# A gated recurrence's units: outputs formed beside the next unit, transposed two units later, preparation in place

## The chip, the cores and the metric

The kernel runs on one core of a Trainium2 chip. The metric is the device time of one execution in microseconds (us); the time before is the median of three runs. One further execution was profiled, and all rows of the profile come from that one.

## What is computed

One layer of a hybrid diffusion backbone over 1024 latent and 256 context tokens: a modulated norm, one input projection, two token mixers beside each other (a bidirectional gated linear recurrence and attention), gates, an output projection, and a feed-forward block. The change touches the recurrence (four heads of 128 keys by 128 values, chunks of 32 tokens, forward and backward):

```python
def hgrn_scan(q, k, v, log_f, s0):               # k = 1 - f, f = exp(log_f)
    a = jnp.cumsum(log_f, axis=3)                # within a chunk of 32 tokens
    a_last = a[:, :, :, -1]
    q_dec = q * jnp.exp(a)
    k_dec = k * jnp.exp(-a)
    scores = jnp.where(mask, jnp.einsum('bhnik,bhnjk->bhnij', q_dec, k_dec), 0.0)
    o_intra = jnp.einsum('bhnij,bhnjv->bhniv', scores, v)
    k_end = k * jnp.exp(a_last[:, :, :, None, :] - a)
    kv = jnp.einsum('bhnck,bhncv->bhnkv', k_end, v)
    decay = jnp.exp(a_last)
    ...                                          # scan over chunks: s = decay * s + kv
    o_inter = jnp.einsum('bhnck,bhnkv->bhncv', q_dec, s_starts)
    o = (o_intra + o_inter)...
    return o, s_final
...
    o = o_f + flip(o_b)                          # both directions
    o = rms_norm(o, norm_w) * jax.nn.silu(heads(hg))
```

The context's scan starts from a zero state, the latents' scans from a given one.

## The kernel before

The stages follow each other: front (norm, q/k/v), attention with a part of the input projection as filler, the recurrence stage with the gate projection as filler (735 to 1077 us in the profile), the merge, the output projection, and the feed-forward block. The order of TensorE's (PE's) instructions is the order in which the code is written; the order on the other engines, and which free buffer a tile gets, is set by a scheduler. An engine carries out its own instructions in order, so one that waits holds all behind it. SyncE (SP) issues nearly all DMAs, also in order.

The recurrence stage is a loop over 24 units (`HUnit`): for each head six pairs of a direction d and a token tile t: (0,0), (0,1), (1,1), (1,0), (0,2), (1,2). Tiles 0 and 1 have 512 tokens (four blocks of 128), tile 2, the context, has 256. Units are counted here from 0, so 6, 12 and 18 begin a head, and the two before each of these are short. A turn of the loop handles unit u:

- `prep` of unit u+1, a turn ahead: loads (`uf` the gate f, `uq`, `uv`, and `ug` for d = 1), k = 1 - f on GpSimd (POOL, L837), two scans on VectorE (DVE, L841 to L846), a dozen tiny products for the chunk factors `um` (L856 to L865), then k times the second scan (POOL, `usf`, L875), the keys `uke` for the state (DVE, L871), the keys for the scores (POOL), and the four scaled queries `uw` (two on DVE, two on POOL).
- `keys_t` (L890): PE transposes `uke`, ScalarE (ACT) copies it to `ukt`. `scores` (L900): 16 or 32 small products, then the mask on DVE (`usm`, L903) and for d = 1 an addition on POOL. `states_` (L911): PE forms kv, DVE chains the states `ust` (L917), four steps for a long unit.
- `out` (L927, L929): PE multiplies the queries `uw` with the states `ust`, and for d = 1 the scores with v. For d = 1, DVE adds the forward part (`uo`, L939), ACT squares, POOL forms the power, and DVE scales (L946). `out_t` (L952): the transpose of `uo`, one unit later in the code.
- Between these stand slices of the filler (`part(x)`): steps of the gate projection (L299 to L301, three products of 512 columns each) and of the modulation (`ada_cols`), whose result DVE adds into `modc` (L190). A unit's slice of the filler is in proportion to its tokens.

Unit u's `ust`, and so its `out`, come in the same turn in which DVE prepares unit u+1. The preparation's tiles lie in ring "X", 20 buffers of 2 KB per partition, 11 or 12 for a unit.

Of the kernel before, what the change touches and what calls it, by code (L numbers as in the profile page):

```python
# [44 lines left out]
def build(ctx, tc, I, O, C):  # L45
# [128 lines left out]
    def ada_cols(pa, ws, cis, ring=None):  # L174
# [8 lines left out]
        s_.activation(ev, pa[:, 0:256], AF.Copy)  # L183

        def late():
            pm = pa[:, 256:260]
            for half, ci in enumerate(cis):
                pe.matmul(pm[:, 2 * half:2 * half + 2], ev[:, half * P:(half + 1) * P], sel, start=True, stop=True)
            for half, ci in enumerate(cis):
                v.tensor_tensor(modc[:, :, ci], pm[:, 2 * half:2 * half + 2],  # L190
                                cols[:, B_ADA + ci:B_ADA + ci + 1].broadcast_to([P, 2]), op=ALU.add)
        return late


# [622 lines left out]
    class HUnit:  # L817
# [6 lines left out]
            self.zero = None if t < 2 else 0 if d == 0 else self.nb - 1  # L824

        def prep(self):
            h, d, t, n, nb = self.h, self.d, self.t, self.n, self.nb
            f, q, vv = S(name="uf"), S(name="uq"), S((P, 4, P), name="uv")
            self.vv = vv
            dma(f[:, 0:n], FD[d][h][t])  # L830
            dma(q[:, 0:n], QD[h][t])
            dma(vv[:, 0:nb, :], VD[h // 2][t][:, :, (h % 2) * P:(h % 2 + 1) * P])
            if d == 1:
                self.gt = S((P, 4, P), name="ug")
                dma(self.gt[:, 0:nb, :], GD[h // 2][t][:, :, (h % 2) * P:(h % 2 + 1) * P])
            k = S(name="uk")
            g_.tensor_scalar(k[:, 0:n], f[:, 0:n], -1.0, 1.0, op0=ALU.mult, op1=ALU.add)  # L837

            c, e = S(name="ucp"), S(name="usf")
            if d == 0:  # L840
                v.tensor_tensor_scan(c[:, 0:n], R[:, 0:n], f[:, 0:n], 1.0, op0=ALU.max, op1=ALU.mult)  # L841
                v.tensor_tensor_scan(e[:, 0:n - 1][:, ::-1], f[:, 1:n][:, ::-1], R[:, 1:n], 1.0, op0=ALU.mult, op1=ALU.max)
                v.memset(e[:, n - 1:n], 1.0)
            else:
                v.tensor_tensor_scan(c[:, 0:n][:, ::-1], R[:, 0:n], f[:, 0:n][:, ::-1], 1.0, op0=ALU.max, op1=ALU.mult)
# [10 lines left out]
            v.tensor_copy(out=Mf[:, 0:nb, 1:12:5], in_=Dv[:, :, 0:3])  # L856
            v.tensor_tensor(Mf[:, 0:nb, 2:8:5], Dv[:, :, 0:2], Dv[:, :, 1:3], op=ALU.mult)
            v.tensor_tensor(M[:, 0:nb, 0, 3], M[:, 0:nb, 0, 2], Dv[:, :, 2], op=ALU.mult)

            v.tensor_copy(out=M[:, 0:nb, 3, 2], in_=Dv[:, :, 3])  # L860
            for cc in (1, 0):
                v.tensor_tensor(M[:, 0:nb, 3, cc], M[:, 0:nb, 3, cc + 1], Dv[:, :, cc + 1], op=ALU.mult)
            v.reciprocal(M[:, 0:nb, 4, :], Dv)
            self.dec = T(4, "udec")
            v.tensor_tensor(self.dec[:, 0:nb], M[:, 0:nb, 3, 0], Dv[:, :, 0], op=ALU.mult)  # L865

            def mul4(out, in0, w, eng):
# [3 lines left out]
                eng.tensor_tensor(out[:, 0:n].rearrange("p (b c i) -> p b c i", c=4, i=32),  # L871
                                  in0[:, 0:n].rearrange("p (b c i) -> p b c i", c=4, i=32),
                                  mm.unsqueeze(3).broadcast_to([P, nb, 4, 32]), op=ALU.mult)
# [33 lines left out]
        def states_(self, st):  # L907
            nb = self.nb
            kv = PS("s", (P, 4, P))
            for b in range(nb):  # L910
                pe.matmul(kv[:, b, :], self.kts[:, b, :], self.vv[:, b, :], start=True, stop=True)  # L911
            self.states = {}
            nxt = S((P, 4, P), name="ust")
            for i, b in enumerate(list(range(nb)) if self.d == 0 else list(range(nb))[::-1]):
                self.states[b] = st
# [1 line left out]
                v.scalar_tensor_tensor(dst, st, self.dec[:, b:b + 1], kv[:, b, :], op0=ALU.mult, op1=ALU.add)  # L917
# [37 lines left out]
            dma(OH[self.h][self.t], e[:, 0:nb].rearrange("p b d -> p (b d)"))  # L955

    def hgrn(fill):
        zs = cp.tile([P, P], F32, name="zs")
        g_.memset(zs, 0.0)
        units = [HUnit(h, d, t) for h in range(4) for d, t in ((0, 0), (0, 1), (1, 1), (1, 0), (0, 2), (1, 2))]  # L960
        st, fwd, late = None, {}, None
        tot = float(sum(u.n for u in units))
        done = 0.0
        units[0].prep()
        for i, u in enumerate(units):
            if i + 1 < len(units):
# [1 line left out]
            if u.t == 2:
                st = zs
            elif u.t == u.d:  # L970
                st = cp.tile([P, P], F32, tag="s0", name="s0", bufs=1)
                dma(st, I["state_hgrn"][u.d, u.h])
            if u.d == 0:
                fwd[u.t] = u
# [15 lines left out]
            if u.t == 2:  # L990
                dma(O["new_state_hgrn"][u.d, u.h], st)
            if u.d == 1:
                late = u
        late.out_t()
# [19 lines left out]
    def with_ada(gens, b0):  # L1014

        for i, gen in enumerate(gens):
            for j, x in enumerate(gen):
                if j == 6 and todo:
                    todo.pop()()
                yield x  # L1020
            if b0 + i < 16:
                raw = wraw(I["w_ada"], KC, 2 * D + (b0 + i) * 256)
                ci = 16 + 2 * (b0 + i)
                todo.append(ada_cols(PS("g"), [lambda k, h=h: raw[:, k, h * P:(h + 1) * P] for h in range(2)], (ci, ci + 1)))
                yield 1.8
# [633 lines left out]
```

## Time and profile before

| | |
|---|---|
| median of three runs | 2169.72 us (2169.2 to 2173.08) |
| profiled execution, its own time | 2168.73 us |
| its span, first to last instruction | 2167.0 us |
| recurrence stage | 735 to 1077 us of the span |
| mean granted TensorE clock | 0.987 |

In rows of the profile, "busy" is the time in which an engine executed, "idle before" the gap ahead of an instruction with what ended it, xN a number of instructions, and L927 a line of the kernel. PEld is PE's weight load, which runs beside its products; PEclk is the share of the full TensorE clock that was granted. Waits are put down to what came last by the semaphore events.

### The profile page before, as it was taken

How to read it: one execution, taken by the hardware profiler on the slowest of the kernel's cores; microseconds unless marked ns; L12 is line 12 of the kernel's file. 1: busy time of each engine (PE TensorE's matmuls, PEld its weight loads, DVE VectorE, ACT ScalarE, POOL GpSimd, SP SyncE). 2: the span in 40 equal slices, each digit the busy share in tenths (PEclk: the TensorE clock that was granted, in tenths of full speed). 3: DMA queues.
4: the chain of work that ended last, by engine and by line, in shares of the span. 5: the costliest groups of instructions: out<-in, count | busy, mean ns of one | idle time of the engine just before them, and what ended most of it. 6: DMA issues, size and time to landing. Idle time of an engine off the chain costs nothing.

```text
span 2167.0 us, 34635 instructions
## 1 busy us (share of the span) xinstructions
PE 2080.5 (96%) x12859; PEld 1789.1 (83%) x12859; DVE 1399.6 (65%) x2668; ACT 954.8 (44%) x1947; POOL 527.6 (24%) x554
## 2 busy tenths in 40 slices
PE   6899999999999999899999999899999999999998
PEld 4788889988899877787888888888888878888876
DVE  3784776677776877678443535966666665666675
ACT  4754555555555522222230425755454444333352
POOL 1472323333333454446212100112111110000010
PEclk9999999999999999999999999999999999999999
DMA  9365121242122344445544333674444478555773
GB/s 283 103 193 158 65 74 39 73 133 69 51 76 69 114 147 148 128 143 164 194 134 136 114 107 116 207 226 141 156 146 151 136 283 269 178 185 172 229 229 104
DMA packets 251065, 316.38 MB, mean 146 GB/s; under 512 B 18168, under 2 KB 171328, under 8 KB 250896
## 3 DMA queue, kind: packets, MB, share of 16 engines
q1 hardware_dynamic: 238768, 274.53, 40.3%
q0 software_dynamic: 12128, 39.64, 5.1%
q8 instruction: 101, 1.65, 0.3%
q14 instruction: 68, 0.56, 0.1%
HBM read 226.55 MB, written 87.56 MB: 145 GB/s over the span
## 4 chain that ended last, share of the span: by engine, by line
PE 75%; DVE 11%; DMA 6%; ACT 3%; issue 3%; SPq 1%; POOL 1%; DVEq 0%; POOLq 0%; ACTq 0%
PE ps_g L299 7%; PE ps_g L300 7%; PE ps_g L301 7%; PE ps_s L658 4%; PE ps_t L699 3%; DMA wraw<-in_w_in 3%; PE ps_s L1479 2%; PE ps_s L1480 2%; PE ps_g L1480 2%; PE ps_s L1481 2%; PE ps_g L1481 2%; PE ps_g L1479 2%; PE ps_s L1317 2%; PE ps_s L1319 2%; PE ps_s L1318 2%
## 5 line engine op out<-in xcount | busy, mean ns | idle before, releaser
L299 PE MATMUL ps_g<-hs,wsp 128*128 128x512 f32 (+1 forms) x960 | 361.0, 376 | 2.5 <-DVE modc L190 2.5
L301 PE MATMUL ps_g<-hs,wsp 128*128 128x512 f32 (+1 forms) x960 | 344.5, 359 | 0.0
L300 PE MATMUL ps_g<-hs,wsp 128*128 128x512 f32 (+1 forms) x960 | 344.3, 359 | 0.0
L677 POOL TENSOR_SCALAR pexp<-pexp,rs 128x512 f32<-128x512 f32 (+1 forms) x104 | 170.1, 1641 | 368.9 <-ACT pTh L702 179.1
L270 ACT ACTIVATE wsp<-wraw 128x1024 fp32r<-128x1024 f32 x118 | 118.2, 1001 | 270.7 <-PE ps_g L300 114.0
L271 DVE TENSOR_TENSOR wsp<-wraw,wsp 128x1024 fp32r<-128x1024 f32 x118 | 140.9, 1194 | 123.5 <-ACT wsp L270 123.1
L299 PEld LDWEIGHTS ps_g<-hs,wsp 128*128 128x128 f32 x960 | 184.0, 192 | 27.6 <-issue 4.8
L301 PEld LDWEIGHTS ps_g<-hs,wsp 128*128 128x128 f32 x960 | 183.5, 191 | 27.8
L300 PEld LDWEIGHTS ps_g<-hs,wsp 128*128 128x128 f32 x960 | 184.4, 192 | 19.9
L702 ACT ACTIVATE pTh<-ps_t 128x512 fp32r<-128x512 f32 x200 | 118.9, 601 | 132.4 <-PE ps_t L699 129.4
L659 DVE TENSOR_REDUCE mx<-ps_s 128x1 f32<-128x512 f32 (+1 forms) x208 | 136.7, 662 | 52.1 <-PE ps_s L658 51.5
L270 ACT ACTIVATE ah<-ar 128x640 fp32r<-128x640 f32 (+1 forms) x112 | 81.0, 723 | 197.6 <-PE ps_g L1451 192.5
L669 ACT ACTIVATE pexp<-ps_s,ngm 128x512 f32<-128x512 f32 (+1 forms) x208 | 137.3, 669 | 45.2 <-DVE ngm L663 43.7
L703 DVE TENSOR_TENSOR pTl<-ps_t,pTh 128x512 fp32r<-128x512 f32 x200 | 135.8, 679 | 13.1 <-ACT pTh L702 12.7
L271 DVE TENSOR_TENSOR ah<-ar,ah 128x640 fp32r<-128x640 f32 (+1 forms) x112 | 89.8, 802 | 74.1 <-ACT ah L270 72.7
L658 PE MATMUL ps_s<-Kl,Ql 128*128 128x512 f32 (+1 forms) x416 | 129.1, 415 | 2.3 <-ACT pexp L669 2.3
L699 PE MATMUL ps_t<-ident,pexp 128*128 128x128 f32 x800 | 120.6, 272 | 3.0 <-DVE pTl L703 1.7
L315 PE MATMUL ps_g<-wsp,hs 128*128 128x256 f32 x400 | 117.1, 293 | 0.0
L316 PE MATMUL ps_g<-wsp,hs 128*128 128x256 f32 x400 | 113.6, 284 | 2.8 <-DVE wsp L271 2.8
L317 PE MATMUL ps_g<-wsp,hs 128*128 128x256 f32 x400 | 113.7, 284 | 0.0
L715 PE MATMUL ps_g<-pTl,Vl 128*128 128x256 f32 x400 | 105.6, 286 | 4.5 <-DVE pTl L703 4.5
L714 PE MATMUL ps_g<-pTh,Vl 128*128 128x256 f32 x400 | 105.5, 284 | 0.2 <-DVE ze L810 0.2
(385 smaller groups left out, 5350.9 us busy)
## 6 DMA issues: line engine op xcount, KB each, us to landing
ar<-AF SPq DMA_DIRECT2D x112, 320.0 KB, 3.3
wraw<-in_w_ff SPq DMA_DIRECT2D x32, 1024.0 KB, 6.0
wr<-in_w_ff SPq DMA_DIRECT2D x128, 256.0 KB, 3.7
wraw<-in_w_in SPq DMA_DIRECT2D x19, 1024.0 KB, 6.5
wraw<-in_w_ada SPq DMA_DIRECT2D x16, 1024.0 KB, 5.4
AF<-a POOLq DMA_DIRECT2D x48, 256.0 KB, 2.7
AF<-t POOLq DMA_DIRECT2D x48, 256.0 KB, 2.3
wa<-in_w_ada SPq DMA_DIRECT2D x32, 256.0 KB, 5.8
```

Of the source, the lines that this page charges most:

```text
L270: s_.activation(hi, raw, AF.Copy)
L271: v.tensor_tensor(lo, raw, f32(hi), op=ALU.subtract)
L299: pe.matmul(out, hi[:, k, :], mh, start=(first and k == 0), stop=False)
L300: pe.matmul(out, hi[:, k, :], ml, start=False, stop=False)
L301: pe.matmul(out, lo[:, k, :], mh, start=False, stop=(last and k == kcs - 1))
L658: pe.matmul(pq[:, 0:n], self.qh[:, q0:q0 + P], K[self.g][var][self.kts[i]], start=(var == 0), stop=(var == 1))
L659: v.tensor_reduce(self.mx[j][:, i:i + 1], pq[:, 0:n], axis=AX.X, op=ALU.max)
L669: s_.activation(e[:, 0:n], self.ps.pop((j, i))[:, 0:n], AF.Exp, bias=self.mx[j], accum_out=self.sm[j][:, i:i + 1])
L677: NORM[(i + j) % len(NORM)].tensor_scalar(x, x, self.rs[j], None, op0=ALU.mult)
L699: pe.transpose(pt[:, a, j * P:(j + 1) * P], self.Ps[j][i][:, b * P:(b + 1) * P], ident)
L702: s_.activation(hi, pt, AF.Copy)
L703: v.tensor_tensor(lo, pt, f32(hi), op=ALU.subtract)
```

## The change

1. `out` of unit u-1 stands behind `states_` of unit u, and `out_t` of unit u-3 just ahead of it; the loop runs three turns longer.
2. `prep` is in place: k overwrites `uf` and is formed on ACT behind both scans; `uke` overwrites `usf`, and so waits for POOL's product that reads it; the fourth query overwrites `uq`. A unit has 8 or 9 tiles in ring "X"; `uv` and `ug` are loaded later in the preparation.
3. The filler is shared by tokens plus 128, and the three extra turns get 300 each, so that less stands between a unit's steps and some stands in the extra turns. The four places of a turn get a quarter each.
4. For the zero state, DVE copies kv in place of a product with a zero tile. The given states have two buffers, `oT` moves to ring "I", and within the two fillers `modc` is added by ACT.

```diff
@@ ada_cols (late) @@
-                v.tensor_tensor(modc[:, :, ci], pm[:, 2 * half:2 * half + 2],
-                                cols[:, B_ADA + ci:B_ADA + ci + 1].broadcast_to([P, 2]), op=ALU.add)
+                if on_act:
+                    s_.activation(modc[:, :, ci], pm[:, 2 * half:2 * half + 2], AF.Identity, bias=cols[:, B_ADA + ci:B_ADA + ci + 1])
+                else:
...
@@ HUnit.prep @@
-            f, q, vv = S(name="uf"), S(name="uq"), S((P, 4, P), name="uv")
+            f, q = S(name="uf"), S(name="uq")
...
-            k = S(name="uk")
-            g_.tensor_scalar(k[:, 0:n], f[:, 0:n], -1.0, 1.0, op0=ALU.mult, op1=ALU.add)
...
+            k = self.k = f
+            s_.activation(k[:, 0:n], f[:, 0:n], AF.Identity, scale=-1.0, bias=1.0)
...
             g_.tensor_tensor(e[:, 0:n], k[:, 0:n], e[:, 0:n], op=ALU.mult)
-            self.ke = S(name="uke")
-            mul4(self.ke, e, 3, v)
             mul4(k, e, 4, g_)
-            self.k = k
+            mul4(e, e, 3, v)
+            self.ke = e
...
-            W[3] = S(name="uw")
-            v.tensor_tensor(W[3][:, 0:n], q[:, 0:n], c[:, 0:n], op=ALU.mult)
+            W[3] = q
+            v.tensor_tensor(q[:, 0:n], q[:, 0:n], c[:, 0:n], op=ALU.mult)
             for w, eng in ((2, g_), (1, g_), (0, v)):
+                if w == 0:
+                    self.vv = S((P, 4, P), name="uv")
+                    dma(self.vv[:, 0:nb, :], VD[h // 2][t][:, :, (h % 2) * P:(h % 2 + 1) * P])
...
@@ HUnit.states_ @@
-                v.scalar_tensor_tensor(dst, st, self.dec[:, b:b + 1], kv[:, b, :], op0=ALU.mult, op1=ALU.add)
+                if b == self.zero:
+                    v.tensor_copy(out=dst, in_=kv[:, b, :])
+                else:
+                    v.scalar_tensor_tensor(dst, st, self.dec[:, b:b + 1], kv[:, b, :], op0=ALU.mult, op1=ALU.add)
@@ hgrn @@
+        N, LATE = len(units), 3
+        share = [u.n + 128.0 for u in units] + [300.0] * LATE
+        tot, done, st = sum(share), 0.0, None
         units[0].prep()
-        for i, u in enumerate(units):
-            if i + 1 < len(units):
+        for i in range(N + LATE):
+            part = lambda x: fill.to((done + x * share[i]) / tot)
+            if i + 1 < N:
                 units[i + 1].prep()
...
-            part = lambda x: fill.to((done + x * u.n) / tot)
-            u.keys_t()
-            part(0.2)
-            u.scores(fwd[u.t])
-            part(0.4)
-            u.states_(st)
-            st = u.last
-            part(0.7)
-            if late is not None:
-                late.out_t()
-                late = None
-            part(0.8)
-            u.out(fwd[u.t])
-            done += u.n
-            fill.to(done / tot)
+            if i < N:
+                u = units[i]
+                u.keys_t()
+                part(0.25)
+                u.scores(u.fwd)
+                part(0.5)
+                u.states_(u.st or st)
+                st = u.last
+                if u.t == 2:
+                    dma(O["new_state_hgrn"][u.d, u.h], st)
+                part(0.75)
+            if i >= LATE and units[i - LATE].d == 1:
+                units[i - LATE].out_t()
+            if 1 <= i <= N:
+                units[i - 1].out(units[i - 1].fwd)
+            part(1.0)
+            done += share[i]
```

PE, unit 10 (the forward context unit of the second head), before: from its kv product (its states go to `ust_11125`) to its own output product in the same turn.

```order
L911 MATMUL ps_s_11122<-uv_10865,ukt_11093 128x128 x2
L299 MATMUL ps_g_11128<-hs_736,wsp_10999 128x512
L300 MATMUL ps_g_11128<-hs_737,wsp_10999 128x512
L301 MATMUL ps_g_11128<-hs_736,wsp_11000 128x512
L299 MATMUL ps_g_11128<-hs_746,wsp_10999 128x512
L300 MATMUL ps_g_11128<-hs_747,wsp_10999 128x512
L301 MATMUL ps_g_11128<-hs_746,wsp_11000 128x512
L299 MATMUL ps_g_11128<-hs_756,wsp_10999 128x512
L300 MATMUL ps_g_11128<-hs_757,wsp_10999 128x512
L301 MATMUL ps_g_11128<-hs_756,wsp_11000 128x512
L952 MATMUL ps_t_11138<-ident_85,uo_11030 128x128 x4
L927 MATMUL ps_g_11146<-ust_11125,uw_10897 128x128
```

PE, the same product now (unit 10's states are `ust_11016` there, L921 is `states_`, L965 `out_t`, L940 `out`, and L302 to L304 are the filler):

```order
L921 MATMUL ps_s_11129<-uv_10952,ukt_11099 128x128 x2
L302 MATMUL ps_g_11026<-hs_714,wsp_11022 128x512
L303 MATMUL ps_g_11026<-hs_715,wsp_11022 128x512
L304 MATMUL ps_g_11026<-hs_714,wsp_11023 128x512
L302 MATMUL ps_g_11142<-hs_736,wsp_11022 128x512
L303 MATMUL ps_g_11142<-hs_737,wsp_11022 128x512
L304 MATMUL ps_g_11142<-hs_736,wsp_11023 128x512
L965 MATMUL ps_t_11146<-ident_85,uo_10888 128x128 x4
L940 MATMUL ps_g_11154<-ust_11016,uw_10806 128x128
```

The kv product ahead of it (`ps_s_11129`) is unit 11's: unit 10's output has moved a whole turn behind its own states.

DVE, the first unit's keys at the start of the stage, before (L703 and L724 belong to the end of attention, L271 to the filler's weights; the row of `uke_9518` is unit 0's keys, `ucp_9537` the first scan of unit 1):

```order
L871 TENSOR_TENSOR uke_9518<-usf_9502,um_9506 128x512
L882 TENSOR_TENSOR uw_9521<-uq_9494,ucp_9501 128x512
L703 TENSOR_TENSOR pTl_9413<-ps_t_9407,pTh_9412 128x512
L724 TENSOR_TENSOR oa_9424<-ps_g_9419,pvt_9425 64x256
L871 TENSOR_TENSOR uw_9527<-uw_9521,um_9506 128x512
L271 TENSOR_TENSOR wsp_9765<-wraw_9574,wsp_9764 128x1024
L724 TENSOR_TENSOR oa_9424<-ps_g_9440,pvt_9445 64x256
L841 SCALAR_TENSOR_TENSOR ucp_9537<-R_9488,uf_9529 128x512
```

DVE now (unit 0's keys are the row that writes `usf_9496`):

```order
L706 TENSOR_TENSOR pTl_9413<-ps_t_9407,pTh_9412 128x512
L865 TENSOR_TENSOR udec_9510<-um_9501,ucp_9495 128x4
L727 TENSOR_TENSOR oa_9424<-ps_g_9419,pvt_9425 64x256
L838 SCALAR_TENSOR_TENSOR ucp_9530<-R_9488,uf_9526 128x512
L839 SCALAR_TENSOR_TENSOR usf_9531<-uf_9526,R_9488 128x511
L840 MEMSET usf_9531 128x1
L274 TENSOR_TENSOR wsp_9759<-wraw_9566,wsp_9758 128x1024
L856 COPY um_9536<-ucp_9530 128x4x3
L857 TENSOR_TENSOR um_9536<-ucp_9530 128x4x2
L727 TENSOR_TENSOR oa_9424<-ps_g_9440,pvt_9445 64x256
L871 TENSOR_TENSOR usf_9496<-usf_9496,um_9501 128x512
```

The keys of unit 0 have moved behind both scans of unit 1 and a weight split.

DVE, the change of head, where unit 6's keys (`usf_10221`) stand now: behind the first scan of unit 7 (`ucp_10327`), which waits for that unit's gate to arrive. Before, each unit's keys stood ahead of the next unit's scan.

```order
L871 TENSOR_TENSOR uw_10247<-uq_10217,um_10226 128x512
L862 TENSOR_TENSOR um_10226<-um_10226,ucp_10220 128x4
L952 TENSOR_TENSOR uo_10188<-ps_g_10179,uo1_9780 128x512
L838 SCALAR_TENSOR_TENSOR ucp_10327<-R_9488,uf_10323 128x512
L163 TENSOR_SCALAR ms_10197<-oss_10190 128x4
L871 TENSOR_TENSOR usf_10221<-usf_10221,um_10226 128x512
```

The keys have moved behind one scan here, at the heads of units 6 and 18; at unit 12 they still stand ahead of the next scan.

More of the change, by code (lines that the diff above doesn't have):

```diff
@@ L172, in build, with ada_cols @@
     v.tensor_reduce(sel, ident.rearrange("p (j r) -> p r j", r=32)[:, 0:2, :], axis=AX.X, op=ALU.add)
-    def ada_cols(pa, ws, cis, ring=None):
+    def ada_cols(pa, ws, cis, ring=None, on_act=False):
         for half in range(2):
@@ L189, in late @@
             for half, ci in enumerate(cis):
-                v.tensor_tensor(modc[:, :, ci], pm[:, 2 * half:2 * half + 2],
-                                cols[:, B_ADA + ci:B_ADA + ci + 1].broadcast_to([P, 2]), op=ALU.add)
+                if on_act:
+                    s_.activation(modc[:, :, ci], pm[:, 2 * half:2 * half + 2], AF.Identity, bias=cols[:, B_ADA + ci:B_ADA + ci + 1])
+                else:
+                    v.tensor_tensor(modc[:, :, ci], pm[:, 2 * half:2 * half + 2],
+                                    cols[:, B_ADA + ci:B_ADA + ci + 1].broadcast_to([P, 2]), op=ALU.add)
         return late
@@ L827, in prep @@
             h, d, t, n, nb = self.h, self.d, self.t, self.n, self.nb
-            f, q, vv = S(name="uf"), S(name="uq"), S((P, 4, P), name="uv")
-            self.vv = vv
+            f, q = S(name="uf"), S(name="uq")
             dma(f[:, 0:n], FD[d][h][t])
             dma(q[:, 0:n], QD[h][t])
[L832 to L835, printed above, removed]
-            k = S(name="uk")
-            g_.tensor_scalar(k[:, 0:n], f[:, 0:n], -1.0, 1.0, op0=ALU.mult, op1=ALU.add)
             c, e = S(name="ucp"), S(name="usf")
@@ L875, in prep @@
             g_.tensor_tensor(e[:, 0:n], k[:, 0:n], e[:, 0:n], op=ALU.mult)
-            self.ke = S(name="uke")
-            mul4(self.ke, e, 3, v)
             mul4(k, e, 4, g_)
-            self.k = k
+            mul4(e, e, 3, v)
+            self.ke = e
             W = self.W = [None] * 4
-            W[3] = S(name="uw")
-            v.tensor_tensor(W[3][:, 0:n], q[:, 0:n], c[:, 0:n], op=ALU.mult)
+            W[3] = q
+            v.tensor_tensor(q[:, 0:n], q[:, 0:n], c[:, 0:n], op=ALU.mult)
             for w, eng in ((2, g_), (1, g_), (0, v)):
+                if w == 0:
+                    self.vv = S((P, 4, P), name="uv")
+                    dma(self.vv[:, 0:nb, :], VD[h // 2][t][:, :, (h % 2) * P:(h % 2 + 1) * P])
+                    if d == 1:
+                        self.gt = S((P, 4, P), name="ug")
+                        dma(self.gt[:, 0:nb, :], GD[h // 2][t][:, :, (h % 2) * P:(h % 2 + 1) * P])
                 W[w] = S(name="uw")
                 mul4(W[w], W[3], w, eng)
+            self.st = None
+            if t == d:
+                self.st = cp.tile([P, P], F32, tag="s0", name="s0", bufs=2)
+                dma(self.st, I["state_hgrn"][d, h])
         def keys_t(self):
@@ L957, in hgrn @@
     def hgrn(fill):
-        zs = cp.tile([P, P], F32, name="zs")
-        g_.memset(zs, 0.0)
         units = [HUnit(h, d, t) for h in range(4) for d, t in ((0, 0), (0, 1), (1, 1), (1, 0), (0, 2), (1, 2))]
-        st, fwd, late = None, {}, None
-        tot = float(sum(u.n for u in units))
-        done = 0.0
+        fwd = {u.h: {} for u in units}
+        for u in units:
+            u.fwd = fwd[u.h].get(u.t)
+            fwd[u.h][u.t] = u
+        N, LATE = len(units), 3
+        share = [u.n + 128.0 for u in units] + [300.0] * LATE
+        tot, done, st = sum(share), 0.0, None
         units[0].prep()
-        for i, u in enumerate(units):
-            if i + 1 < len(units):
+        for i in range(N + LATE):
+            part = lambda x: fill.to((done + x * share[i]) / tot)
+            if i + 1 < N:
                 units[i + 1].prep()
[L968 to L974, printed above, removed]
-            part = lambda x: fill.to((done + x * u.n) / tot)
-            u.keys_t()
-            part(0.2)
-            u.scores(fwd[u.t])
-            part(0.4)
-            u.states_(st)
-            st = u.last
-            part(0.7)
-            if late is not None:
-                late.out_t()
-                late = None
-            part(0.8)
-            u.out(fwd[u.t])
-            done += u.n
-            fill.to(done / tot)
[L990 to L994, printed above, removed]
+            if i < N:
[15 more added lines that the diff above has]
+            done += share[i]
     GT = [[DR((P, n), "GT%d_%d" % (c, t)) for t, (_, n, _) in enumerate(TT)] for c in range(16)]
@@ L1023, in with_ada @@
                 ci = 16 + 2 * (b0 + i)
-                todo.append(ada_cols(PS("g"), [lambda k, h=h: raw[:, k, h * P:(h + 1) * P] for h in range(2)], (ci, ci + 1)))
+                todo.append(ada_cols(PS("g"), [lambda k, h=h: raw[:, k, h * P:(h + 1) * P] for h in range(2)], (ci, ci + 1), on_act=True))
                 yield 1.8
```

2 rows, old and new, of the table RING_OF are left out of this document.

## The prediction

> **What bounds the kernel now.** First the busy shares, then the waits of the recurrence stage, where alone the orders of the two kernels differ by more than `modc`'s engine.
>
> ```profile
> PE 2080.5 (96%) x12859; PEld 1789.1 (83%) x12859; DVE 1399.6 (65%) x2668; ACT 954.8 (44%) x1947; POOL 527.6 (24%) x554
> ```
>
> PE is the bound; time comes only from its gaps and its clock. The waits of PE from 735 to 1080 us (total, times, longest):
>
> ```profile
> PE ps_g L927 <- DVE ust L917: 16.7, 13, 4.4
> PE ps_g L299 <- DVE modc L190: 2.5, 1, 2.5
> ...
> PE ps_t L952 <- DVE uo L946: 1.7, 1, 1.7
> PE ps_s L911 <- ACT ukt L892: 0.9, 1, 0.9
> ```
>
> The output products wait for states that DVE has not chained. Three of the thirteen, in PE's timeline:
>
> ```profile
> 849.22 1.22 PE L927 MATMUL ps_g<-ust,uw 128*128 128x128 f32 x4 [4.43 <-DVE ust L917]
> 851.06 0.80 PE L927 MATMUL ps_g<-ust,uw 128*128 128x128 f32 x2 [0.62 <-DVE ust L917]
> ...
> 909.18 0.49 PE L927 MATMUL ps_g<-ust,uw 128*128 128x128 f32 x2 [1.36 <-DVE ust L917]
> ...
> 918.78 0.80 PE L927 MATMUL ps_g<-ust,uw 128*128 128x128 f32 x2 [2.42 <-DVE ust L917]
> ```
>
> DVE around the first of them:
>
> ```profile
> 843.00 1.62 DVE L845 TENSOR_TENSOR_SCAN ucp<-R,uf 128x512 f32<-128x512 f32 x1
> ...
> 848.83 0.33 DVE L917 SCALAR_TENSOR_TENSOR ust<-s,udec,ps_s 128x128 f32<-128x128 f32 x1
> ...
> 851.53 0.34 DVE L917 SCALAR_TENSOR_TENSOR ust<-ust,udec,ps_s 128x128 f32<-128x128 f32 x1
> ```
>
> From 843.00 to 848.83 DVE prepares unit 7; only then does it chain unit 6's states, for an output product due in the same turn. DVE is late by its order, not by its load: 249.73 us in the stage, below. PE busy, PEld, DVE, ACT, POOL, then the granted clock, of the stage and of the stretches behind the longer gaps:
>
> ```profile
> 735.00:1077.00 342.00, 317.26 (x2522) 268.03 (x2521) 249.73 (x567) 83.53 (x212) 158.47 (x174) 0.97 0.48 151
> 768.00:774.00 6.00, 6.00 (x28) 4.95 (x28) 5.89 (x12) 1.79 (x3) 4.02 (x4) 0.72 0.47 138
> 783.00:789.00 6.00, 4.59 (x15) 3.57 (x15) 2.60 (x5) 1.19 (x2) 3.19 (x5) 0.72 0.44 145
> 846.00:858.00 12.00, 8.16 (x25) 6.57 (x26) 7.21 (x20) 1.19 (x2) 5.69 (x6) 0.57 0.47 141
> 918.00:924.00 6.00, 5.22 (x26) 4.96 (x27) 5.90 (x12) 1.43 (x5) 4.35 (x5) 0.72 0.42 124
> 999.00:1005.00 6.00, 5.66 (x40) 4.35 (x44) 5.86 (x17) 1.18 (x5) 3.53 (x3) 0.72 0.51 152
> ```
>
> So a gap costs twice: itself, and PE's work behind it at a lower clock. Busy time times (1 - clock) gives 1.7 + 1.3 + 3.5 + 1.5 + 1.6 = 9.6 us. That agrees with the whole stage, 0.03 x 317.26 = 9.5.
>
> **The change, part by part.** The sum is made against the profiled execution's 2168.73 us; the median, 2169.72, is 0.99 above it.
>
> *Output a turn later.* Between a unit's states and its output product now stand a turn's keys, scores, states and filler: 342 us over 24 units is 14 us a turn on average, and the longest lateness seen is 4.43. I take all 16.7 away. What is late next on DVE would be the keys, below.
>
> *Transpose two units later.* The one such wait is the last, where nothing is left to cover the chain from the output to `uo`:
>
> ```profile
> 1072.96 0.61 PE L929 MATMUL ps_g<-uv,usm 128*128 128x128 f32 x4
> ...
> 1076.32 0.59 PE L952 MATMUL ps_t<-ident,uo 128*128 128x128 f32 x2 [1.67 <-DVE uo L946]
> ```
>
> ```profile
> L299 PE MATMUL ps_g<-hs,wsp 128*128 128x512 f32 (+1 forms) x336 | 132.7, 395 | 2.5 <-DVE modc L190 2.5
> ```
>
> The chain takes 1076.32 - 1072.96 = 3.4 us. The three extra turns hold 900 of 14,212 shares, 6.3% of the stage's filler; two lie between the last output and its transpose, 4.2%. The filler's first products alone are busy for 132.7 us, and two more follow each; 4.2% of these alone is 5.6 us, more than 3.4. The 1.7 goes.
>
> *`modc` on ACT.* The 2.5 us wait was for a small addition behind a scan:
>
> ```profile
> 995.25 1.23 DVE L271 TENSOR_TENSOR wsp<-wraw,wsp 128x1024 fp32r<-128x1024 f32 x1 [1.53 <-ACT wsp L270]
> ...
> 997.95 1.19 DVE L842 TENSOR_TENSOR_SCAN usf<-uf,R 128x511 f32<-128x511 f32 x1
> 999.07 0.15 DVE L190 TENSOR_TENSOR modc<-ps_g,cols 128x2 f32<-128x2 f32 x1
> ...
> 999.21 0.16 DVE L856 COPY um<-ucp 128x12 f32<-128x12 f32 x1
> 999.28 0.16 DVE L857 TENSOR_TENSOR um<-ucp 128x8 f32<-128x8 f32 x1
> ```
>
> On ACT, busy 83.53 of 342 us, it no longer stands behind scans. The 2.5 goes; on ACT the 32 small operations cost at most the 0.38 of an eviction each (752.80, below), a share of what ACT has idle.
>
> Removed: 16.7 + 1.7 + 2.5 = 20.9, and the clock behind these gaps, 9.6: 30.5.
>
> *The start.* Here something new lands on the path. Unit 0's keys stand now behind both scans of unit 1 and a weight split. Before, on DVE:
>
> ```profile
> 747.91 0.69 DVE L871 TENSOR_TENSOR uke<-usf,um 128x512 f32<-128x512 f32 x1
> ...
> 749.84 0.41 DVE L724 TENSOR_TENSOR oa<-ps_g,pvt 64x256 f32<-64x256 f32 x1
> ...
> 750.86 2.07 DVE L271 TENSOR_TENSOR wsp<-wraw,wsp 128x1024 fp32r<-128x1024 f32 x1
> ...
> 753.42 1.23 DVE L841 TENSOR_TENSOR_SCAN ucp<-R,uf 128x512 f32<-128x512 f32 x1
> 754.56 1.20 DVE L842 TENSOR_TENSOR_SCAN usf<-uf,R 128x511 f32<-128x511 f32 x1
> ```
>
> and on ACT and PE:
>
> ```profile
> 752.80 0.38 ACT L183 ACTIVATE ev<-ps_g 128x256 f32<-128x256 f32 x1 [0.44 <-DMA uv<-VD]
> ...
> 753.23 0.61 PE L188 MATMUL ps_g<-sel,ev 128*128 128x2 f32 x4 [0.55 <-ACT ev L183]
> 753.70 0.63 PE L890 MATMUL ps_t<-ident,uke 128*128 128x128 f32 x4
> ```
>
> In the new order: 749.84 + 0.41 = 750.25; scans 1.23 + 1.20; the split 1.23 (995.25) to 2.07 (750.86); two small operations, 0.16 each (999.21, 999.28), up to 0.4; an eviction 0.41; the keys 0.69: 755.3 to 756.3. PE, there at 753.70, waits 1.6 to 2.6; ACT's eviction behind k ends within that time. I take 2.2, nearer the split that ran 2.07, and 1.7 of clock, as behind 2.42 at 768: 3.9. Ends: 1.6 without clock loss, 2.6 + 1.7 = 4.3.
>
> *Head changes.* At units 6 and 18 the keys stand behind a scan that waits for its gate. Before, one such load and its scan:
>
> ```profile
> 828.01 5.42 DMA uf<-FD
> ...
> 833.46 1.22 DVE L841 TENSOR_TENSOR_SCAN ucp<-R,uf 128x512 f32<-128x512 f32 x1 [2.93 <-DMA uf<-FD]
> ```
>
> ```profile
> uf<-FD SPq DMA_DIRECT2D x16, 256.0 KB, 2.8
> ```
>
> The median load lands after 2.8 us and the slow one after 5.42. The load's turn is a short one, 384 of 14,212 shares of some 317 us: 8.6 us (an estimate, as if all of PE's work went by shares). Ahead of the load SP has the state's store, which follows the last state; the states above took 2.7 us from first to last beside other work, so I put the issue 1 to 2.7 us into the turn. With 2.8 for the load, 1.22 for the scan and 0.69 for the keys there is room (5.7 to 7.4); with 5.42 the keys end at 8.3 to 10.0, up to 1.4 late, and up to 2 with small operations between. I take the middle, 1.0 twice: 2.0. Ends 0 and 4.0, the latter with 1.5 of clock each: 7.
>
> *At no cost.* k moves from POOL to ACT:
>
> ```profile
> L837 POOL TENSOR_SCALAR uk<-uf 128x512 f32<-128x512 f32 (+1 forms) x24 | 18.3, 764 | 17.9 <-PE ps_t L890 15.2 <-DMA uf<-FD 2.1 <-PE ps_g L927 0.5
> ```
>
> ```profile
> L871 POOL TENSOR_TENSOR uk<-usf,um 128x512 f32<-128x512 f32 (+1 forms) x24 | 25.1, 1046 | 3.5 <-DVE um L863 1.1 <-DVE um L862 0.9 <-DVE um L858 0.3
> ```
>
> ```profile
> L892 ACT ACTIVATE ukt<-ps_t 128x512 f32<-128x512 f32 (+1 forms) x24 | 12.5, 520 | 24.3 <-PE ps_t L890 24.3
> ```
>
> By the ACT row, nearest in size and engine, it takes about 0.52 x 24 = 12.5 us of ACT's 258 idle. Since k overwrites the gate, it must follow both scans, so POOL's first product comes up to one ACT operation later; POOL loses 18.3 us of its own and the scans free the gate's tile sooner. What is queued behind k on ACT is rival D. The keys in place wait for POOL's product that reads the same tile, 1.05 us more a unit; that lies in the preparation, a turn ahead of `keys_t`, and if that cover goes it adds to the head changes only. The fourth query in place removes no instruction. The copies for the zero state replace 8 steps of the kind that took 0.33 (848.83); even at that price nothing changes. Fewer tiles in ring "X" (9 against 12 of 20 buffers) let two units' tiles stand at once, so SP's loads are issued earlier; `uv` and `ug`, issued later, are read only by `states_` and `uo`, well over a turn behind. Two buffers for given states and `oT` in ring "I" can only delay a load or a store, which nobody on PE waits for in the rows above. Filler by length plus 128 gives the short turns more: 384 against 256 of their old share, where the work per token was thinnest.
>
> *Sum.* -20.9 - 9.6 + 3.9 + 2.0 = -24.6; 2168.73 - 24.6 = 2144.1, and with 0.99 for the median 2145.
>
> [...] Rows first: the gap of 2.42 at 918.78 and that of 2.5 ahead of 999 stand at the head of stretches with 0.72. [...]
>
> **The rivals.**
>
> A, the forecast, 0.52: 2145. Its own range: 1.6 for the start and none at heads gives 2145 - 2.3 - 2.0 = 2140.7; 4.3 and 7 give 2150.4. The waits for ACT that I left alone (0.9, and 0.55 at 753.23) widen this: gone, with 1.7 of clock, 2137.5; doubled, 2152.
>
> B, the waits come back as `keys_t` waiting for DVE at the changes of head, 0.26. For it: the keys now stand behind scans, and at 828 a gate took 5.42 us. Against it: DVE has 92 us idle in the stage. Three changes at 2.42 plus 1.6 of clock are 12.1 instead of 2.0: 2155. Three at the worst seen, 4.43 + 0.62 + 3.5 = 8.55 each, 25.7: 2168.7.
>
> C, the clock does not follow such gaps, 0.05: the low clock at 768, 783, 918 and 999 (1.7 + 1.3 + 1.5 + 1.6 = 6.1) stays, and the start costs no clock, 1.7: 2145 + 6.1 - 1.7 = 2149.4.
>
> D, slower, 0.11: k on ACT waits for DVE's second scan, and `ukt`, the filler's evictions (`ze`) and `ev`, which PE needs, stand behind it. One mechanism, once a unit. It decides where it costs PE more than 24.6 / 24 = 1.0 us a unit. For it: PE waited for ACT's `ukt` once already, 0.9 us. Against it: both scans stand back to back, so ACT waits at most 1.2 to 1.6 us, and PE was seen to wait for ACT in two places only, 0.9 and 0.55. At 2.0 us a unit: 48 - 24.6 = 23.4 above, 2193.
>
> E, no change, 0.06: the recurrence's chain through the preparation (loads, scans, POOL's products, keys), not the output, sets the turn, and the wait only moves from L927 to the keys' transposes: 2165 to 2173. Against it: those transposes don't appear in the waits at all.
>
> **How the numbers follow.** About 0.2%, 4 us, is what a measurement here can tell from none. A, B's larger part and C are faster: 0.52 + 0.26 + 0.05 = 0.83; E, and no more, is the same: 0.06; D is slower: 0.11. The range 2136 to 2166 holds A, C and all of B but its last 3 us (I put 0.03 there): 0.80.
>
> **What would show it.** Right: no `ust` row among PE's waits, one gap of about 2 us at the first keys' transposes, the stage near 317 us and its clock at 0.99 or above. Wrong: rows of the keys' transposes waiting for the keys or of `ps_t` at units 6, 12 and 18 (B); an unchanged 0.97 with the gaps gone (C); PE waiting for ACT in most turns (D). The prediction is most exposed where one late gate holds DVE, since all that DVE does stands behind it.

## The result, and the profile after

| | before | changed |
|---|---|---|
| median | 2169.46 us (2167.5 to 2173.08, four runs) | 2154.11 us (2150.08 to 2155.36, four runs) |
| ratio | | 0.9925, 95% interval 0.9911 to 0.9938 |
| profiled span | 2167.0 us | 2148.0 us |

The change is faster by 15.4 us in the medians, 0.75%. Forecast were 24.6 less, 2145; the time lies in the range, and a little under two thirds of the gain came. Run again beside the experiments, the same kernel had 2150.28 us, ratio 0.9903 (0.9887 to 0.992). The page of the changed kernel, busy time by engine:

```profile
PE 2070.8 (96%) x12859; PEld 1781.9 (83%) x12859; DVE 1388.4 (65%) x2636; ACT 971.2 (45%) x2003; POOL 504.0 (23%) x529
```

PE is still the bound, with the same 12,859 products. Its waits from 735 to 1080 us (total, times, longest):

```profile
PE ps_g L302 <- DVE uo L952: 7.0, 2, 4.6
PE ps_s L921 <- ACT ukt L902: 3.7, 3, 1.5
PE ps_t L900 <- DVE usf L871: 1.6, 1, 1.6
PE ps_g L718 <- DVE pTl L706: 1.3, 2, 1.1
PE ps_g L940 <- ACT ze L1011: 1.2, 1, 1.2
```

The `ust` row of before (16.7), the `modc` row (2.5) and that of the last transpose (1.7) are gone. In their place stand rows that were absent or smaller before: the filler (L302) waits for DVE to read an output (`uo`, L952), `states_` (L921) waits 3.7 for ACT's `ukt` (0.9 before), and the output product (L940) waits for ACT's `ze`.

To say where the time lies, three marks in PE's timeline serve: the first attention product that waits in the last block, the first transpose of keys, and the first product of the merge. Of before and of the changed kernel, the last two:

```profile
753.70 0.63 PE L890 MATMUL ps_t<-ident,uke 128*128 128x128 f32 x4
...
1104.30 0.40 PE L299 MATMUL ps_s<-hs,wsp 128*128 128x512 f32 x1
```

```profile
753.29 0.66 PE L900 MATMUL ps_t<-ident,usf 128*128 128x128 f32 x4 [1.62 <-DVE usf L871]
...
1085.56 0.40 PE L302 MATMUL ps_s<-hs,wsp 128*128 128x512 f32 x1
```

From keys to merge it was 350.60 us and is 332.27: 18.3 less. The stretch before it, from 743.34 of before and 738.94 of the changed kernel to the first keys, was 10.36 and is 14.35: 4.0 more. Together 14.3 less, against a forecast of 24.6. Of the signs that the prediction named, no `ust` row and one gap of about 2 us at the first keys (1.6) came; the stage is shorter by 14.3 and not by some 25, and from keys to merge its clock is 0.98, not 0.99.

Of the remaining 4.7 of the two spans' 19.0, 4.4 lie ahead of these marks, in the front and in attention, and 0.3 behind the merge. They can't be put down to the change: over the 14 executions profiled here the front's end varied from 187.1 to 192.6 us, the changed kernel itself giving 188.1 and 192.2, and attention's length from 549.4 to 553.5. One part of the change does act in attention, `modc` on ACT. Attention took 552.6 us on average in the three executions with this addition on DVE (`before`, `late_only`, `late_po`: 551.5 to 553.5) and 550.7 in the eleven with it on ACT (549.4 to 553.4). Some 2 us may be gained there; the ranges overlap, so this is not shown.

### The profile page after: what moved, and what is told of

Read it like the earlier page. It is cut to its first block, busy times and chain, and to the rows that moved or that the text cites. A ratio compares the mean times of both kernels' runs of the same rounds, so it can differ in the third digit from the quotient of the medians.

```text
span 2148.0 us, 34607 instructions
## 1 busy us (share of the span) xinstructions
PE 2070.8 (96%) x12859; PEld 1781.9 (83%) x12859; DVE 1388.4 (65%) x2636; ACT 971.2 (45%) x2003; POOL 504.0 (23%) x529
## 4 chain that ended last, share of the span: by engine, by line
PE 79%; DVE 9%; DMA 6%; ACT 4%; issue 2%; SPq 1%; POOL 0%; DVEq 0%; POOLq 0%; ACTq 0%
PE ps_g L302 8%; PE ps_g L303 8%; PE ps_g L304 8%; PE ps_s L661 4%; PE ps_t L702 4%; PE ps_s L1487 2%; PE ps_s L1488 2%; PE ps_s L1489 2%; PE ps_g L1488 2%; PE ps_g L1489 2%; PE ps_s L1325 2%; PE ps_s L1327 2%; PE ps_g L1487 2%; PE ps_s L1326 2%; PE ps_g L718 2%; PE ps_g L318 2%
## 5 line engine op out<-in xcount | busy, mean ns | idle before, releaser
L302 PE MATMUL ps_g<-hs,wsp 128*128 128x512 f32 (+1 forms) x960 | 357.7, 373 | 7.1 <-DVE uo L952 7.0
L304 PE MATMUL ps_g<-hs,wsp 128*128 128x512 f32 (+1 forms) x960 | 342.6, 357 | 0.0
L302 PEld LDWEIGHTS ps_g<-hs,wsp 128*128 128x128 f32 x960 | 182.2, 190 | 32.6 <-DVE uo L952 7.5
L304 PEld LDWEIGHTS ps_g<-hs,wsp 128*128 128x128 f32 x960 | 181.9, 190 | 27.2
```

Source lines behind the costliest of these rows:

```text
L302: pe.matmul(out, hi[:, k, :], mh, start=(first and k == 0), stop=False)
L304: pe.matmul(out, lo[:, k, :], mh, start=False, stop=(last and k == kcs - 1))
```

## The experiments

Twelve kernels ran, in three groups, each beside the kernel before. The table has for each the time, and from its profile the stretch ahead of the first keys ("start"), from there to the merge ("units"), and their sum. The sum is the better measure of an edit to the recurrence: it leaves out the front and attention. It comes from one execution each, and the two executions of the changed kernel differ by 1.6, so kernels whose sums lie within some 2 us are not told apart by it.

| kernel | median us | ratio (95%) | start | units | sum |
|---|---|---|---|---|---|
| before | 2169.46 | 1 | 10.4 | 350.6 | 361.0 |
| changed | 2154.11 | 0.9925 (0.9911 to 0.9938) | 14.3 | 332.3 | 346.6 |
| `again` | 2150.28 | 0.9903 (0.9887 to 0.992) | 14.3 | 330.6 | 345.0 |
| `k_pool` | 2155.26 | 0.9925 (0.9909 to 0.9941) | 14.3 | 332.4 | 346.7 |
| `keys_own` | 2160.34 | 0.9953 (0.9937 to 0.9969) | 11.9 | 338.4 | 350.3 |
| `same_turn` | 2190.54 | 1.0092 (1.0073 to 1.0112) | 14.3 | 365.5 | 379.8 |
| `late_only` | 2152.25 | 0.9914 (0.9897 to 0.993) | 10.4 | 334.8 | 345.2 |
| `share_tok` | 2153.88 | 0.9924 (0.9907 to 0.994) | 14.3 | 330.2 | 344.5 |
| `po_s` | 2145.86 | 0.9889 (0.9872 to 0.9906) | 14.3 | 325.0 | 339.4 |
| `first_own` | 2148.74 | 0.9907 (0.989 to 0.9925) | 12.0 | 332.4 | 344.4 |
| `po_s_first` | 2140.98 | 0.9877 (0.9863 to 0.989) | 12.3 | 322.9 | 335.2 |
| `po_s_first_mid` | 2142.37 | 0.9885 (0.9869 to 0.9902) | 11.9 | 320.8 | 332.7 |
| `late_po` | 2148.49 | 0.9909 (0.9893 to 0.9925) | 10.4 | 328.5 | 338.9 |
| `late_po_act` | 2147.0 | 0.9897 (0.9884 to 0.9911) | 10.4 | 326.8 | 337.2 |

### Are the new waits the kernel's, or one execution's?

> The changed kernel once more, as the measure for the edits beside it. Theory 1 (what was given back sits at fixed places: ACT behind k, POOL ahead of the keys in place): 2150 to 2156 us, and the profile again shows the uo waits of the filler (7.0 in the first profile), ukt (3.7) and the first keys (1.6) at the same places. Rival (these waits are accidents of one execution): the same time, the waits at other places or of other sums.

The waits of a second execution:

```profile
PE ps_g L302 <- DVE uo L952: 6.8, 2, 4.5
PE ps_s L921 <- ACT ukt L902: 3.9, 3, 1.7
PE ps_t L900 <- DVE usf L871: 1.9, 1, 1.9
```

7.0, 3.7 and 1.6 before, 6.8, 3.9 and 1.9 now, at the same instructions. They belong to the kernel.

### k back on POOL

```diff
-            s_.activation(k[:, 0:n], f[:, 0:n], AF.Identity, scale=-1.0, bias=1.0)
+            g_.tensor_scalar(k[:, 0:n], f[:, 0:n], -1.0, 1.0, op0=ALU.mult, op1=ALU.add)
```

> The changed kernel with k = 1 - f formed on POOL, still in place behind both scans. Theory 1: the waits for ukt (3.7), for ze (1.2) and the uo wait of 4.6 behind a late weight load go, with the clock behind two of them (1.6 and 2.2): 13 less, 2141, and at least 2147 if POOL's 18 to 24 us of new work delay the keys. Rival 1 (ACT's place does not matter, DVE's load sets the stage): 2150 to 2156 with other waits of the same sum. Rival 2 (POOL becomes late): above 2156, with PE waiting for keys or usm.

Theory 1 missed; the time is that of the changed kernel, as rival 1 has it. The waits now:

```profile
PE ps_g L302 <- DVE uo L952: 9.2, 2, 6.0
PE ps_s L921 <- ACT ukt L902: 2.5, 3, 1.5
```

The `ze` row is gone with k on ACT, but `uo` waits longer and part of `ukt` stays. What holds `ukt` is seen in the changed kernel's ACT, and ahead of it in DVE and PE, at one of the three places. PE finishes an output's products (L940, L942) at about 883.6; DVE reads them here:

```profile
883.39 1.25 DVE L858 TENSOR_TENSOR um<-um,ucp 128x4 f32<-128x4 f32 x1
...
884.84 1.34 DVE L871 TENSOR_TENSOR uw<-uq,um 128x512 f32<-128x512 f32 x1
886.10 1.01 DVE L862 TENSOR_TENSOR um<-um,ucp 128x4 f32<-128x4 f32 x1
887.03 0.33 DVE L930 SCALAR_TENSOR_TENSOR ust<-ust,udec,ps_s 128x128 f32<-128x128 f32 x1
887.29 0.68 DVE L952 TENSOR_TENSOR uo<-ps_g,uo 128x512 f32<-128x512 f32 x1
```

and ACT's squares of it follow, with a weight copy and only then `ukt`, for which PE waits 1.48:

```profile
888.06 0.31 ACT L956 ACTIVATE ojk<-uo 128x128 f32<-128x128 f32 x1 [4.83 <-DVE uo L952]
...
889.25 1.04 ACT L273 ACTIVATE wsp<-wraw 128x1024 fp32r<-128x1024 f32 x1
890.20 0.36 ACT L902 ACTIVATE ukt<-ps_t 128x256 f32<-128x256 f32 x1
```

```profile
890.61 0.71 PE L921 MATMUL ps_s<-uv,ukt 128*128 128x128 f32 x4 [1.48 <-ACT ukt L902]
```

ACT had been idle for 4.83 us, waiting for `uo`. So the lateness is DVE's reading of the output, behind a later unit's preparation, and it reaches PE by two ways: ACT's queue (squares ahead of `ukt`) and the filler's PSUM ring "g", of three buffers, one of which the output holds. The third `ukt` wait, 0.81 at 963.31, is of the same kind. k on ACT is the cause at the second: at 927.56 k, after 5.85 us idle, stands just ahead of `ukt`, for which PE waits 1.41. It is also the cause of the `ze` wait:

```profile
977.18 0.63 ACT L847 ACTIVATE uf<-uf 128x512 f32<-128x512 f32 x1 [8.58 <-DVE usf L844]
977.72 0.37 ACT L1011 ACTIVATE ze<-ps_g 128x256 f32<-128x256 f32 x1
```

```profile
978.14 0.49 PE L940 MATMUL ps_g<-ust,uw 128*128 128x128 f32 x2 [1.22 <-ACT ze L1011]
```

Both of these waits, 1.41 and 1.22, are absent in `k_pool`; others took their place. That the output is read late became theory 2.

### The keys in their own tile

```diff
-            mul4(k, e, 4, g_)
-            mul4(e, e, 3, v)
-            self.ke = e
+            self.ke = S(name="uke")
+            mul4(self.ke, e, 3, v)
+            mul4(k, e, 4, g_)
```

> The changed kernel with the keys for the state in a tile of their own, ahead of POOL's product, as before the change. Theory 1: the first keys stand ahead of unit 1's scans again, so the start's 4.0 goes (1.6 gap, 1.0 ahead of it, 1.5 of clock), and so does the uo wait of 2.4 with 1.3 of clock: 2154 - 7.7 = 2146. Rival (ring X with one tile more a unit is late again, or the places only move): 2152 or more.

The time, 2160.34, is the rival's. Of theory 1 half held: the start is 11.9, 2.4 shorter. But from keys to merge it is 6 to 8 us longer, and `uo` waits 10.4 in place of 7.0, `ukt` 4.9 in place of 3.7. So keys in place are worth something here. Why is open; that one tile more a unit makes the preparation later was not tried by itself.

### The output in its own turn again

```diff
-            if 1 <= i <= N:
-                units[i - 1].out(units[i - 1].fwd)
+            if i < N:
+                units[i].out(units[i].fwd)
```

> The changed kernel with each unit's output in the turn of its own states, as before; all else as changed. Theory 1 (the turn between states and output is what removed 16.7 us of gaps and some 8 of clock): 2166 to 2178, with the ust row back among PE's waits at 10 or more. Rival (the earlier preparation and the filler's new shares removed them): 2150 to 2158, ust row below 3.

The output's move is the mechanism. Without it the rest of the change is slower than the kernel before, by 0.92% (0.73% to 1.12%), beyond the range that I gave:

```profile
PE ps_g L940 <- DVE ust L930: 18.2, 16, 3.3
PE ps_g L940 <- DVE ust L928: 12.9, 4, 4.9
```

31.1 us of `ust` waits, against 16.7 before the change. That the earlier preparation pushes the states further back on DVE would explain it; no run separates that from the other edits.

### The output's move alone

The kernel before, with the loop of the change (outputs of unit u-1 behind `states_` of unit u, transposes of u-3, three more turns), and nothing else of it.

> The kernel before with one part of the change: the output one turn after its states and the transpose two units later, three more turns, no filler in them; preparation, filler shares and k as before. Theory 2 (the output's move takes the ust waits away; what is late next is DVE's reading of the output, uo, behind the preparation, and 12 tiles a unit in ring X leave the preparation later still): ust below 2, uo and keys waits of 10 or more in their place, 2156 to 2170. Rival (the move alone is the whole gain): 2147 to 2154. Rival 2 (without the preparation in place it is slower than before): above 2172.

The rival had it right: the move alone (of outputs and transposes) is the whole gain, 0.9914 against 0.9925 and 0.9903. Its waits:

```profile
PE ps_g L299 <- DVE modc L190: 5.4, 1, 5.4
PE ps_t L952 <- DVE uo L946: 3.8, 1, 3.8
PE ps_s L911 <- ACT ukt L892: 2.7, 2, 2.1
...
PE ps_g L299 <- ACT uo L936: 1.5, 1, 1.5
PE ps_g L299 <- DVE uo L939: 0.7, 1, 0.7
```

There is no `ust` row, and no row shows harm from twelve tiles a unit in ring "X". What the other parts gain (no 5.4 for `modc`, no 3.8 at the last transpose) they give back at the start (4.0) and in longer `uo` waits (7.0 on DVE against 0.7; with the forward outputs that ACT reads, 7.2 against 2.2).

### The filler's shares

```diff
-        share = [u.n + 128.0 for u in units] + [300.0] * LATE
+        share = [u.n + 0.0 for u in units] + [0.0] * LATE
```

> The changed kernel with the filler shared by tokens alone and none in the three last turns. Theory 2: the short units' turns get shorter, so uo is read later against PE there, and the last transpose has no cover: 4 to 10 longer than the changed kernel, 2155 to 2162. Rival (the shares do nothing): 2149 to 2153.

The time is within the changed kernel's. The last transpose waits 3.83 (it had none in the changed kernel), and the `uo` row is gone, with `ze` at 3.0 in its place. So the shares move waits and leave the sum where it was (344.5): theory 2 missed, but that they do nothing isn't true either.

### The output's PSUM ring

```diff
-            po = PS("p", (P, 4, P))
+            po = PS("s", (P, 4, P))
```

> The changed kernel with the output's product in PSUM ring s (that of scores and kv) in place of ring g (the filler's). Theory 2: the filler no longer waits for DVE to read the output, so the 7.0 of L302 and the clock behind them, 3.5, go: 2152 - 10 = 2142; ukt's waits stay. Rival (the lateness is DVE's, and the next user of the buffer waits as long): 2148 or more, with scores or kv waiting for uo.

The time, 2145.86, lies between the two; by the waits it is theory 2:

```profile
PE ps_s L921 <- ACT ukt L902: 6.1, 4, 3.0
PE ps_t L900 <- DVE usf L871: 2.0, 1, 2.0
```

No product waits for `uo` any more; `ukt` grew from 3.7 to 6.1. The growth is at the place behind k: 2.96 there, where ACT waits 7.41 us for DVE's second scan, against 1.41 in the changed kernel, and 1.34 at a new place. The sum of start and units fell by 7.2 (346.6 to 339.4; by 5.6 against `again`).

### The first unit's keys alone

The keys' own tile of `keys_own`, under the condition `h == 0 and d == 0 and t == 0`.

> The changed kernel with a tile of its own for the first unit's keys alone. Theory 1 for the start: its stretch from the last attention blocks to the first keys was 14.3 in four executions and 11.9 with all keys in their own tiles; here 11.9 too and the rest as in the changed kernel, 2152 - 2.5 = 2149.5. Rival (the order downstream shifts and gives it back): 2152 or more.

The start is 12.0, 2.3 shorter, as forecast, and the units are those of the changed kernel at 332.4. By the whole time (0.9907 against 0.9903 and 0.9925) it can't be told from the changed kernel.

### Both edits, and two ways on

> The changed kernel with the two edits that gained: the output's product in PSUM ring s, and a tile of its own for the first unit's keys. If their gains add up (6 and 2.4 of the start): 2143, with the start at 11.9 and no uo row. Rival (the orders shift and they don't add): 2146 or more.

They add: sum 335.2, 11.4 under the changed kernel and 25.8 under before, ratio 0.9877. By the whole time it is the best version here. That it lies near where the prediction had put the change, 24.6 under before, is a coincidence of sizes. The longest row of its waits:

```profile
PE ps_s L925 <- ACT ukt L906: 6.1, 4, 3.0
```

Half of the 6.1 is one wait of 3.00 at 921.47, and there k, not a square, stands ahead of `ukt`, after 7.44 us in which ACT waits for DVE's second scan:

```profile
920.52 0.42 ACT L847 ACTIVATE uf<-uf 128x256 f32<-128x256 f32 x1 [7.44 <-DVE usf L840]
920.84 0.58 ACT L906 ACTIVATE ukt<-ps_t 128x512 f32<-128x512 f32 x1
```

So theory 3, below, names the cause of about half of this row. k on POOL together with ring "s" and the whole preparation in place was not run.

The next kernel moves `out` of unit u-1 between `scores` and `states_` of unit u:

> The same, and the previous unit's output stands between this unit's scores and its states, so that ACT's squares of it come well ahead of the next unit's ukt. Theory 3 (what is left, ukt at 6.1, is ACT's squares waiting for a late uo ahead of ukt): ukt below 2 and 2136 to 2142. Rival (uo is read between scores and states, where DVE has the mask and the preparation too, so that the states come late): 2145 or more, with kv, states or scores waited for.

```profile
PE ps_s L944 <- DVE ust L934: 4.2, 3, 2.8
...
PE ps_s L925 <- ACT ukt L906: 1.0, 1, 1.0
```

`ukt` falls from 6.1 to 1.0, also at the place behind k, where PE now comes later; so this does not tell the squares from k. `ust` comes back with 4.2, since the output now stands 3 to 8 us nearer to its states. By the sum it is 2.5 shorter, hardly more than two executions of one kernel differ by; by the whole time (0.9885) it is no different.

The two last kernels have the output's move and ring "s", but not the rest of the change; the second has `modc` on ACT too.

> The kernel before with the output's move and the output's product in ring s; preparation, k, shares and modc as before. Theory 3 (the preparation in place, k on ACT and the filler's shares bring nothing together): as the changed kernel with ring s, 2143 to 2150, with the modc wait (5.4) and the last transpose (3.8) still there. Rival (they pay once the filler's ring is free): 2151 or more.

> The same with modc added by ACT within the two fillers, as in the change. If the modc wait is its place behind DVE's scans: 5.4 less and 3 to 4 of clock behind it, some 7 below the one without. Rival (the wait only moves): within 3 of it. A gain or a loss in the attention stage, ahead of the recurrence, would show there: 551 us in all executions so far, within 2.

`late_po` has a sum of 338.9, and `po_s`, with all of the change, 339.4: the preparation in place, k on ACT and the shares together bring nothing, with the filler's ring free too, because what they save among the units (325.0 against 328.5) they lose at the start (14.3 against 10.4). With the start mended (`po_s_first`, 335.2) they are worth 3.7, and 2.0 beside `late_po_act`, which is within what two executions differ by. The last transpose waits 3.8 in both, as expected. The 5.4 of `modc` were gone already with the ring (its row is missing in both), so that the addition on ACT had nothing to gain in the recurrence: 337.2 against 338.9, within 3. Attention took 550.8 us in `late_po_act` and 552.9 in `late_po`, the difference spoken of above.

## Why the prediction was right, and where it was off

*The output a turn later, 16.7: right.* No row of `ust` is left, undoing it brings 31.1 back, and doing it alone, with the transposes' move, gives the whole gain. One reading was off, without effect on the sum: the scan at 843.00 (L845) is one of the backward direction, so DVE was preparing unit 8 there and not unit 7, two units ahead of the states that it kept waiting.

*The last transpose, 1.7: right.* The wait is absent, and 3.83 without filler in the last turns (`share_tok`, `late_only`): the cover of 5.6 us or more was enough.

*`modc`, 2.5: gone, but not shown to be ACT's doing.* With the addition on DVE the wait was 5.4 in `late_only` and none in `late_po`; with it on ACT, `again` and `first_own` have a wait of 0.8 for `modc`.

*The start, 3.9: right in size, in part by luck.* It cost 4.0. The wait for the keys is 1.62, at the low end of 1.6 to 2.6, and `first_own`, which puts these keys back, takes 2.3 off. The clock that I priced behind this wait was not lost there but ahead of it, behind waits of 1.04 for `oa` at 742.62, which I had not priced, and 1.11 for `pTl` at 744.09:

```profile
744.00:747.00 3.00, 2.90 (x16) 2.61 (x16) 2.94 (x6) 0.61 (x2) 1.81 (x2) 0.72 0.19 67
753.00:756.00 3.00, 2.71 (x14) 2.35 (x15) 2.97 (x8) 0.60 (x1) 2.54 (x4) 1.00 1.07 359
```

`first_own` still has the 1.03 for `oa` and a clock of 0.63 from 744.70 to 747.70. So the term came out by the sum of two things, one of them not the keys'.

*Head changes, 2.0: right place, wrong mechanism, undersized.* I priced keys that come late for their transposes at the heads of units 6 and 18. There the keys were not late: they were done at 817.5 and 964.5, and PE transposes them at 820.70 and 967.31. PE's two longest new waits stand just behind those turns, at the start of turns 7 and 19, for the context unit's output of the turn before:

```profile
837.44 0.79 PE L302 MATMUL ps_g<-hs,wsp 128*128 128x512 f32 x1 [2.40 <-DVE uo L952]
...
986.63 0.79 PE L302 MATMUL ps_g<-hs,wsp 128*128 128x512 f32 x1 [4.57 <-DVE uo L952]
```

The second is behind DVE's own work, the preparation, the states and a weight split:

```profile
985.01 1.22 DVE L274 TENSOR_TENSOR wsp<-wraw,wsp 128x1024 fp32r<-128x1024 f32 x1
986.15 0.42 DVE L952 TENSOR_TENSOR uo<-ps_g,uo 128x256 f32<-128x256 f32 x1
```

PE's products for this output end at about 979; DVE works from 974.81 to 986.15 almost without a pause before it reads them. The weights are late too (ACT's copy of them, which the split needs, ends at 984.98), but they are not what held `uo`: in `k_pool` that copy was done at 984.90, DVE came to the split only at 986.11, and PE waited 6.00.

The step that failed is "What is late next on DVE would be the keys": the output's own reader is on DVE too, and moved with it into the thick of a preparation. It costs 7.0 and clock instead of 2.0.

*"At no cost", ACT: wrong by 4.0.* `ukt` 3.7 and `ze` 1.2, where I had left 0.9. It is rival D's queue: k on ACT, waiting for DVE's second scan, accounts for 1.41 of `ukt` and for the `ze` wait of 1.22, and the squares of a late output for the other 2.29 of `ukt`. But it struck in four places, not once a unit, so that D's outcome never came near.

*The clock.* Of 10.5 us of PE's work times the clock lost (before, in windows of 0.2 us from the keys to the merge; the longer windows of the prediction give 9.6), 5.6 were left in this execution and 3.0 in `again`, besides 1.7 at the start in each; I had the 1.7 at the start and nothing at the heads. Rival C keeps four of the five low stretches of before and drops only the one behind the gap of 4.43; that its length sets this gap apart no run shows. The changed kernel has three low stretches from keys to merge, with gaps of 2.40, 1.48 and 4.57.

In sum, of PE's waits between keys and merge 22.1 went and 12.1 came; the clock gave 4.9; with the start's 4.0 that makes 10.9 of the 14.3 measured. The other 3.4 have no wait in the trace. They are PE's busy time, which fell from 328.4 to 320.2 between keys and merge, by 3.3 more than the clock's part. The 128 output products on `ust` alone went from 26.6 us busy to 22.0, in part the clock's again; the rest stays open.

## What to carry to other kernels

When a product is moved away from its late operand, ask who reads its result, in which queue, and which ring of PSUM buffers it holds until then: here the reader was on the very engine that had been late, and the filler stopped for the buffer. Give such a result a ring that the filler does not share (5.6 to 7.2 us of the stage here). And try the part that carries the mechanism alone: the other edits of this change summed to nothing as it stands.

## What the hardware showed

The clock's loss is not a function of the gap. In the changed kernel the gap of 2.40 that ends at 837.44, and so short a one as the 1.48 that ends at 890.61, were followed by half the clock:

```profile
837.60:840.60 3.00, 3.00 (x35) 2.06 (x35) 2.36 (x7) 1.32 (x6) 0.81 (x2) 0.50 0.26 62
892.20:895.20 3.00, 2.98 (x11) 2.18 (x10) 3.00 (x4) 2.10 (x6) 1.45 (x1) 0.50 0.00 0
```

In `again` the same two gaps, 2.25 and 1.39, cost nothing:

```profile
839.00:845.00 6.00, 4.57 (x49) 3.57 (x50) 5.11 (x16) 1.98 (x7) 0.81 (x2) 1.00 0.37 107
891.00:897.00 6.00, 4.14 (x22) 3.39 (x23) 5.60 (x8) 3.06 (x8) 3.11 (x3) 1.00 0.24 90
```

In this stage the loss came in pieces of one size. Read in windows of 0.2 us, the clock is 1.00 or 0.50, but for the windows that hold an edge. The five low stretches of `before` (from 768.3, 785.5, 846.9, 918.5 and 1000.5) lasted 3.42, 3.42, 10.24, 3.41 and 3.41 us, the four of the changed kernel (from 745.2, 837.4, 892.0 and 984.2) 3.42, 3.42, 3.41 and 6.83: one, two or three pieces. So the 0.72 of the prediction's windows of 6 us is one such piece: 3.42 of 6 us at half the clock. One piece takes up to 1.7 us of PE's work, half of 3.42.

The two executions are of one kernel. So a term for the clock behind gaps of 1.4 to 2.5 us is a chance of such a piece, not a sum: 10.5 before, 5.6 and 3.0 for one and the same kernel after.

Some small operations on DVE took here as long as POOL's product beside them. One of 128 by 4 numbers took 1.25 from 883.39, to the end of POOL's product; the next such one took 0.16 at 884.56, where it began just ahead of POOL's next product (884.58):

```profile
883.32 1.31 POOL L875 TENSOR_TENSOR usf<-uf,usf 128x512 f32<-128x512 f32 x1 [5.54 <-ACT uf L847]
```

```profile
884.56 0.16 DVE L862 TENSOR_TENSOR um<-um,ucp 128x4 f32<-128x4 f32 x1
```

The long one and POOL's product end at 884.64 and 884.63. It is not the only one: from 735 to 1086 us of the changed kernel 28 operations that the timeline lists singly, of 128 by 4 to 12 numbers, took 0.42 to 1.26 us. POOL had an instruction running beside each, and 24 of them ended 0.01 to 0.04 us behind the end of one. Why, no run here tests. Such stretches stand ahead of the late `uo` above (1.25, 1.34 and 1.01 there), and I had not priced them.
